# Seven half-size block products in the place of eight in the down projections of two MLPs

## The chip, the cores and the metric

One Trainium2 chip, one core of it. The metric is device time in microseconds (us), the median of the runs. The engines are named as the profile names them: PE is TensorE (PEld its weight loads), DVE is VectorE, ACT is ScalarE, POOL is GpSimd, SP is the engine that issues the DMAs.

## What is computed

Two decoder layers over 512 tokens of width 1024, all in float32. Each layer ends with an MLP of hidden width 4096, and a layer norm behind it:

```python
def sqrelu_mlp(x, w_up, w_down):
    return jnp.square(jax.nn.relu(x @ w_up)) @ w_down
...
        x = layer_norm(ALPHA * x + mix, ln_gain[layer, 0], ln_bias[layer, 0])
        x = layer_norm(ALPHA * x + sqrelu_mlp(x, mlp_w_up[layer], mlp_w_down[layer]), ln_gain[layer, 1], ln_bias[layer, 1])
```

Attention and its projections stand before the MLP; the change does not touch their arithmetic.

## The kernel before, in words

A matrix product of two float32 matrices is made of three: each operand is split as `hi + lo` (`hi` is the value rounded to float32r by ScalarE, `lo = value - hi` by VectorE or GpSimd), and PE adds `hi*hi`, `hi*lo` and `lo*hi` up in one bank of PSUM. A bank holds 128 partitions x 512 float32; there are four tags of two banks each (`g`, `o`, `s`, `t`).

Weights come from DRAM in units of 128 x 1024 numbers (512 KB): `unit` (L131) loads one into `wraw` (two buffers), ScalarE writes `whi` (L145), VectorE writes `wlo` (L146; in the attention parts GpSimd does it, by `lo_engine`). `whi` and `wlo` have four buffers each.

The MLP (`mlp`, L363) works in two halves of the hidden width. In a half, eight chunks of 256 hidden columns are computed by `tr_block` (L183): the weights are loaded into PE and the 512 tokens are the moving side, so a matmul is 512 wide (L191 to L193), and its output has the hidden columns on partitions. ScalarE applies relu (L377), VectorE squares (L378), ScalarE and VectorE split the result into `hh` and `hl` (L114, L116). Then the down projection goes over four chunks of 256 output columns: `hh` or `hl` of 128 tokens is loaded into PE and the weights are the moving side, 256 wide (L396 to L398). VectorE adds each finished bank to the residual `y` (L403, L405). The last chunk of the second half is computed token block by token block, each followed by its layer norm (`layer_norm`, L205), so that norm and output of one block run beside the matmuls of the next.

The order of the work on each engine is set by a scheduler of the framework from the program; every engine works its own queue in that order. A tile that takes the buffer of an older one waits until the older one's readers are done.

Of the kernel before, what the change touches and what calls it, by code (L numbers as in the profile page):

```python
# [8 lines left out]
F32 = mybir.dt.float32  # L9
F32R = mybir.dt.float32r  # L10
AF = mybir.ActivationFunctionType
ALU = mybir.AluOpType
# [40 lines left out]
# offsets in the tile of constants  # L53
# [7 lines left out]
def tile_trunk(ctx: ExitStack, tc: tile.TileContext, x, xt_in, ln_gain, ln_bias, w_up, w_down, w_ie, w_oe, lam_p, subln,  # L61
# [50 lines left out]
    def split(src, hi, lo, scale=1.0):  # L112
        """hi + lo = scale * src, exactly; hi and lo are float32r"""
# [15 lines left out]
    lo_engine, rope_engine = [V], [V]  # L129

    def unit(flat, off, nk, w, pl=None, parts=1):  # L131
        """one [128 nk x w] block of a weight matrix as hi and lo [128, nk, w]"""
# [5 lines left out]
        if pl is None:  # L138
            hi = new(wp, "whi", [P, UW], F32R, bufs=4)
            lo = new(wp, "wlo", [P, UW], F32R, bufs=4)  # L140
        else:
            hi, lo = pl[:, :UW], pl[:, UW:]
        for a in range(0, n, n // parts):
            c = slice(a, a + n // parts)
            A.activation(hi[:, c], raw[:, c], AF.Copy)  # L145
            lo_engine[0].tensor_tensor(lo[:, c], raw[:, c], hi[:, c].bitcast(F32), op=ALU.subtract)  # L146
        return (hi[:, :n].rearrange("p (k c) -> p k c", k=nk), lo[:, :n].rearrange("p (k c) -> p k c", k=nk))

    class Weights:
# [3 lines left out]
        def take(self, w, pl=None, nk=4, parts=1):  # L153
            u = unit(self.flat, self.off, nk, w, pl, parts)
# [3 lines left out]
        def chunk(self, w, *pls, parts=1):  # L158
            """all 8 row blocks of w columns: list of (hi, lo) [128, w]"""
            r = []  # L160
            for i, nk in enumerate((4, 4) if w <= 256 else (3, 3, 2)):
                h, l = self.take(w, pls[i].rearrange("p a c -> p (a c)") if pls else None, nk=nk, parts=parts)
# [3 lines left out]
    def nat_chunk(us, w, evac):  # L166
        """[512 x w] = x @ W chunk, tokens on partitions; evac(bank view [128, n, w], first token block, n)"""
# [15 lines left out]
    def tr_block(us, nb, cuts=(0, SEQ)):  # L183
        """[128 x 512] = (x @ W)^T for the nb-th 128 columns of a chunk"""
# [45 lines left out]
    def stacks_q(ap, b, scale):  # L230
        """from [128 = two heads x 64, 512]: per head the stack of hi and lo parts"""
# [766 lines left out]
```

## Time and profile before

| what | us |
|---|---|
| median of 3 runs | 1328.76 |
| the runs | 1325.63, 1328.76, 1329.45 |
| span of the profiled execution | 1325.2 |
| PE busy in it | 1288.5 |
| DVE busy | 735.7 |
| ACT busy | 557.1 |
| POOL busy | 302.1 |
| four down stretches, 92 each | 368 |

The profiled execution has no time of its own beside its span; the runs, which include what lies around the span, are 0.4 to 4.2 us longer than it. Busy time of PE is from its matmuls' modelled ends, which overlap: the pace of PE is read from the starts of successive matmuls, not from the mean duration of one. For DVE likewise: where two instructions stand without a wait between them, the second starts some 0.08 us before the first one's end.

### The profile page before, as it was taken

The page shows a single profiled execution, that of the slowest core. Times are in us where ns is not written, and L with a number is a line of the kernel's source. Part 1 is how long each engine was busy: PE and PEld are TensorE (multiplying, and loading weights), DVE is VectorE, ACT ScalarE, POOL GpSimd, SP SyncE. Part 2 cuts the span into 40 slices and gives each one's busy share as a digit, 9 for nine tenths or more (in the row PEclk, how much of TensorE's full clock was granted, in tenths as well). Part 3 has the DMA queues.
Part 4 walks back from the last instruction along what each step waited for, and adds up shares of the span by engine and source line. Part 5 has one row for each costly group of instructions (what it writes and reads, how often), then busy time and mean ns, then how long its engine had stood idle before and what let it go on. Part 6 is the DMA issues. An engine that isn't in the chain of part 4 may idle for free.

```text
span 1325.2 us, 21558 instructions
## 1 busy us (share of the span) xinstructions
PE 1288.5 (97%) x8726; PEld 1188.8 (90%) x8726; DVE 735.7 (56%) x1466; ACT 557.1 (42%) x1049; POOL 302.1 (23%) x321
## 2 busy tenths in 40 slices
PE   8999998999999999999999999999999999999997
PEld 7999896988888999889997888989988899888997
DVE  4467778787544233443347788877944422344334
ACT  5257767753344112332213566765334311233220
POOL 1135554454000000000034445555500000000003
PEclk9999998999999999999999999999999999999999
DMA  7321011212322222222323323242323232223321
GB/s 273 121 80 49 33 48 33 95 61 84 111 97 96 93 84 95 96 96 96 123 78 128 97 82 94 89 151 65 130 87 102 96 96 90 85 95 96 101 92 64
DMA packets 38578, 125.35 MB, mean 95 GB/s; under 512 B 4672, under 2 KB 5184, under 8 KB 38480
## 3 DMA queue, kind: packets, MB, share of 16 engines
q1 hardware_dynamic: 38480, 123.99, 28.2%
q8 instruction: 68, 1.11, 0.4%
q14 instruction: 30, 0.25, 0.1%
HBM read 119.75 MB, written 4.23 MB: 94 GB/s over the span
## 4 chain that ended last, share of the span: by engine, by line
PE 88%; DVE 7%; ACT 2%; issue 1%; DMA 1%; POOL 1%; SPq 0%; DVEq 0%; ACTq 0%
PE g L193 11%; PE g L191 10%; PE g L192 10%; PE o L398 9%; PE o L397 9%; PE o L396 9%; PE g L178 4%; PE g L179 4%; PE g L180 4%; PE t L285 3%; PE s L267 2%; PE s L268 2%; PE o L301 1%; PE o L300 1%; PE g L353 1%; PE t L550 1%
## 5 line engine op out<-in xcount | busy, mean ns | idle before, releaser
L145 ACT ACTIVATE whi<-wraw 128x1024 fp32r<-128x1024 f32 (+2 forms) x180 | 188.5, 1049 | 288.4 <-PE o L398 223.4
L146 DVE TENSOR_TENSOR wlo<-wraw,whi 128x1024 fp32r<-128x1024 f32 (+1 forms) x129 | 158.7, 1231 | 213.7 <-ACT whi L145 213.7
L398 PE MATMUL o<-whi,hl 128*128 128x256 f32 x928 | 262.3, 283 | 0.0
L397 PE MATMUL o<-wlo,hh 128*128 128x256 f32 x928 | 262.2, 283 | 0.0
L396 PE MATMUL o<-whi,hh 128*128 128x256 f32 x928 | 261.0, 283 | 0.0
L192 PE MATMUL g<-big,wlo 128*128 128x512 f32 x608 | 237.5, 391 | 0.0
L191 PE MATMUL g<-big,whi 128*128 128x512 f32 x608 | 237.3, 390 | 0.0
L193 PE MATMUL g<-big,whi 128*128 128x512 f32 x608 | 237.2, 390 | 0.0
L146 POOL TENSOR_TENSOR wlo<-wraw,whi 128x1024 fp32r<-128x1024 f32 (+2 forms) x51 | 123.7, 2430 | 429.3 <-ACT whi L145 417.0
L397 PEld LDWEIGHTS o<-wlo,hh 128*128 128x128 f32 x928 | 178.2, 192 | 0.2
L398 PEld LDWEIGHTS o<-whi,hl 128*128 128x128 f32 x928 | 178.2, 192 | 0.0
L396 PEld LDWEIGHTS o<-whi,hh 128*128 128x128 f32 x928 | 177.4, 192 | 0.2
L193 PEld LDWEIGHTS g<-big,whi 128*128 128x128 f32 x608 | 114.2, 188 | 23.6
L191 PEld LDWEIGHTS g<-big,whi 128*128 128x128 f32 x608 | 114.2, 188 | 23.1 <-issue 0.2
L192 PEld LDWEIGHTS g<-big,wlo 128*128 128x128 f32 x608 | 114.1, 188 | 23.0
L178 PE MATMUL g<-whi,big 128*128 128x256 f32 (+2 forms) x416 | 120.4, 289 | 0.8 <-DVE fz L809 0.4
L180 PE MATMUL g<-whi,big 128*128 128x256 f32 (+2 forms) x416 | 119.5, 287 | 0.0
L179 PE MATMUL g<-wlo,big 128*128 128x256 f32 (+2 forms) x416 | 119.1, 286 | 0.0
L378 DVE TENSOR_TENSOR h<-h 128x512 f32<-128x512 f32 x64 | 44.3, 692 | 125.5 <-ACT h L377 125.5
L272 ACT ACTIVATE p<-p,sm 128x128 f32<-128x128 f32 (+3 forms) x160 | 89.2, 558 | 46.8 <-DVE sm L271 45.6
L377 ACT ACTIVATE h<-g 128x512 f32<-128x512 f32 x64 | 38.2, 597 | 164.8 <-PE g L193 164.8
L210 POOL TENSOR_TENSOR ve<-ve,nhalf 128x1 f32<-128x1 f32 x16 | 15.9, 992 | 361.2 <-DVE ve L209 361.2
(249 smaller groups left out, 2530.3 us busy)
## 6 DMA issues: line engine op xcount, KB each, us to landing
wraw<-w_up SPq DMA_DIRECT2D x64, 512.0 KB, 3.3
wraw<-w_down SPq DMA_DIRECT2D x64, 512.0 KB, 3.3
wraw<-w_io SPq DMA_DIRECT2D x22, 512.0 KB, 3.5
wraw<-w_ie SPq DMA_DIRECT2D x18, 512.0 KB, 3.7
v<-w SPq DMA_DIRECT2D x8, 512.0 KB, 5.2
wraw<-w_oe SPq DMA_DIRECT2D x8, 512.0 KB, 3.5
cb<-c_dram SPq DMA_DIRECT2D x16, 256.0 KB, 3.3
wraw<-w_oo SPq DMA_DIRECT2D x8, 512.0 KB, 3.6
```

The source lines that it names most:

```text
L145: A.activation(hi[:, c], raw[:, c], AF.Copy)
L146: lo_engine[0].tensor_tensor(lo[:, c], raw[:, c], hi[:, c].bitcast(F32), op=ALU.subtract)
L178: T.matmul(bv[:, tt], xh, h, start=first, stop=False)
L179: T.matmul(bv[:, tt], xh, l, start=False, stop=False)
L180: T.matmul(bv[:, tt], xl, h, start=False, stop=last)
L191: T.matmul(b[:, a:e], h[:, cs], xh, start=k == 0, stop=False)
L192: T.matmul(b[:, a:e], l[:, cs], xh, start=False, stop=False)
L193: T.matmul(b[:, a:e], h[:, cs], xl, start=False, stop=k == 7)
L272: A.activation(pv, pv, AF.Exp, bias=sm[:, i:i + 1], scale=-1.0, accum_out=sm[:, 4 + i:5 + i])
L396: T.matmul(bvs[t], hh[:, ts_], us[0][:, f], start=first, stop=False)
L397: T.matmul(bvs[t], hh[:, ts_], us[1][:, f], start=False, stop=False)
L398: T.matmul(bvs[t], hl[:, ts_], us[0][:, f], start=False, stop=lst)
```

## The change

The hidden width is now worked in four groups of 1024 columns (two blocks `m` of 512) in the place of two halves. In a group, the product `hidden (512 tokens x 1024) @ W (1024 x 1024)` is cut in 2 x 2: tokens 0-255 and 256-511, the first and second 256 hidden columns of each block `m`, output columns 0-511 and 512-1023. The eight half-size block products that this takes become seven, each of a sum or difference of blocks of the hidden values (`left`) and a sum of blocks of the weights (`right`), and the seven results are added to and subtracted from the four quarters of `y` (`evac`). A half-size product is 24 matmuls, each 512 wide on the weights' side. Products are named by their number in the code, in the order 3, 5, 7, 6, 1, 2, 4.

The hidden values stay unsplit in a tile of the tag `big`; every product has its left side split anew (`hsplit`), and its right side (`wsplit`). Raw weights are kept in a new tag `wdr` (eight buffers, the whole of a group), loaded in pieces of 512. GpSimd forms the sums of weights, some of the updates of `y`, and the `lo` of every second unit of the up weights; nothing else of the up projection is changed but the buffers of its first chunk. The last group leaves products 2 and 4 to the end, norms tokens 0-255 ahead of them and 256-511 behind them.

```diff
     def mlp(mp, wu, wd, us0, ln, last):
...
+                us = us0 if m == 0 and j == 0 else wu.chunk(256, engs=(V, G))
...
-                    split(h, hh, hl)
-                    hT.append((hh, hl))
...
+        def wsplit(r):
+            hi = new(wp, "whi", [P, UW], F32R, bufs=4)
+            lo = new(wp, "wlo", [P, UW], F32R, bufs=4)
+            A.activation(hi, r, AF.Copy)
+            V.tensor_tensor(lo, r, hi.bitcast(F32), op=ALU.subtract)
...
+            def left(r):
+                hi = new(mp, "sh", [P, 2, 2, 256], F32R, bufs=3)
+                lo = new(mp, "sl", [P, 2, 2, 256], F32R, bufs=3)
+                for m in range(2):
+                    (h11, h12), (h21, h22) = H[m]
+                    if r == 5:
+                        src = new(mp, "t1", [P, 2, 256], bufs=1)
+                        V.tensor_tensor(src, h12, h11, op=ALU.subtract)
+                    elif r == 7:
+                        src = t3[m] = new(mp, "t3", [P, 2, 256], bufs=2)
+                        V.tensor_tensor(src, h22, h12, op=ALU.subtract)
...
+                    hsplit(hi[:, m], lo[:, m], src)
...
+            def right(r):
...
+                    if r == 5:
+                        src = new(mp, "wds", [P, UW], bufs=2)
+                        G.tensor_tensor(src, w["21", m], w["22", m], op=ALU.add)
+                    elif r == 7:
+                        src = w["22", m]
+                        G.tensor_tensor(src, src, w["12", m], op=ALU.add)
+                    elif r == 6:
+                        src = w["21", m]
+                        G.tensor_tensor(src, src, w["22", m], op=ALU.add)
+                    elif r == 1:
+                        src = w["21", m]
+                        G.tensor_tensor(src, src, w["11", m], op=ALU.add)
...
+            def product(r, lf, us, tt):
...
+                        T.matmul(bv, hh, us[m][0][:, k], start=first, stop=False)
+                        T.matmul(bv, hh, us[m][1][:, k], start=False, stop=False)
+                        T.matmul(bv, hl, us[m][0][:, k], start=False, stop=lst)
...
+                elif r == 6:
+                    e, f = ef[tt]
+                    V.tensor_tensor(f, f, b, op=ALU.add)
+                    V.tensor_tensor(e, e, b, op=ALU.subtract)
+                    G.tensor_tensor(y12, y12, f, op=ALU.add)
+                    add(y22, f, eng=G)
+                    add(y11, e, eng=G)
...
+            for r in (3, 5, 7, 6, 1) if end else (3, 5, 7, 6, 1, 2, 4):
+                lf, us = left(r), right(r)
+                for tt in range(2):
+                    evac(r, product(r, lf, us, tt), tt)
...
+        for g in range(4):
+            hs = [up(2 * g + m) for m in range(2)]
+            down(g, hs, g == 3)
```

In the first group of a layer `add` gives the updates of `y22` and `y11` to VectorE in the place of GpSimd, since they carry the factor ALPHA.

What this makes of the queues is shown at three places. First VectorE's queue in a down projection. Before, in layer 0 (`wlo` is the low part of a weight unit, `big` the residual, `o` a bank):

```order
L146 TENSOR_TENSOR wlo_5200<-wraw_5197,whi_5199 128x1024
L146 TENSOR_TENSOR wlo_5254<-wraw_5251,whi_5253 128x1024
L403 SCALAR_TENSOR_TENSOR big_3658<-big_3658,o_4919 128x256 x2
L403 SCALAR_TENSOR_TENSOR big_3661<-big_3661,o_4920 128x256 x2
L146 TENSOR_TENSOR wlo_5308<-wraw_5305,whi_5307 128x1024
L146 TENSOR_TENSOR wlo_5368<-wraw_5365,whi_5367 128x1024
L146 TENSOR_TENSOR wlo_5422<-wraw_5419,whi_5421 128x1024
L146 TENSOR_TENSOR wlo_5476<-wraw_5473,whi_5475 128x1024
L403 SCALAR_TENSOR_TENSOR big_3658<-big_3658,o_5141 128x256 x2
```

Now, in layer 1, group 1, from the second half of product 6's update to the last weight split of the down projection (`f`, `e` are sums of products, `sl` the low part of a left side, `wdr` raw weights or their sum, `t` a bank):

```order
L501 TENSOR_TENSOR f_10899<-f_10899,o_10987 128x512
L502 TENSOR_TENSOR e_10846<-e_10846,o_10987 128x512
L411 TENSOR_TENSOR sl_11092<-t_1938_10903,sh_11091 128x512
L411 TENSOR_TENSOR sl_11092<-t_1939_10907,sh_11091 128x512
L406 TENSOR_TENSOR wlo_11018<-wdr_10789,whi_11017 128x1024
L406 TENSOR_TENSOR wlo_11056<-wdr_10799,whi_11055 128x1024
L406 TENSOR_TENSOR wlo_11060<-wdr_10801,whi_11059 128x1024
L406 TENSOR_TENSOR wlo_11100<-wdr_10795,whi_11099 128x1024
L508 TENSOR_TENSOR big_9252<-big_9252,t_11021 128x512
L508 TENSOR_TENSOR big_9252<-big_9252,t_11035 128x512
L406 TENSOR_TENSOR wlo_11104<-wdr_10797,whi_11103 128x1024
```

Before, four units of weights and two pairs of updates took turns; now there are sums, splits of left sides, splits of weights and updates in one row, and the last weight split (row 11) stands behind two updates that wait for PE and for GpSimd.

Second GpSimd's queue, in the same group and up to the next up projection (L455 forms the right side of product 1, L503 and L481 update `y`, L446 and L449 form right sides of the next group, L146 is the low part of an up unit). Before, GpSimd had nothing to do in an MLP until its final layer norm:

```order
L455 TENSOR_TENSOR wdr_10789<-wdr_10789,wdr_10801 128x1024
L503 TENSOR_TENSOR big_9252<-big_9252,f_10884 128x512
L481 TENSOR_TENSOR big_9255<-big_9255,f_10884 128x512
L481 TENSOR_TENSOR big_9252<-big_9252,e_10830 128x512
L503 TENSOR_TENSOR big_9252<-big_9252,f_10899 128x512
L481 TENSOR_TENSOR big_9255<-big_9255,f_10899 128x512
L481 TENSOR_TENSOR big_9252<-big_9252,e_10846 128x512
L446 TENSOR_TENSOR wds_11473<-wdr_11401,wdr_11405 128x1024
L446 TENSOR_TENSOR wds_11479<-wdr_11403,wdr_11407 128x1024
L449 TENSOR_TENSOR wdr_11405<-wdr_11405,wdr_11409 128x1024
L449 TENSOR_TENSOR wdr_11407<-wdr_11407,wdr_11411 128x1024
L146 TENSOR_TENSOR wlo_11145<-wraw_11142,whi_11144 128x1024
```

The second half of the next group's first up unit is now split behind four sums for the next down projection.

Third PE's queue in the same group, from the second weight block of product 1 on (`t` is a bank of product 1, `s` of product 2, `o` of product 4; before, a down projection was 384 matmuls 256 wide, block by block, with no such heads drawn ahead):

```order
L469 MATMUL t_11021<-whi_11017,sh_11005 128x512
L469 MATMUL t_11035<-whi_11017,sh_11005 128x512
L469 MATMUL s_11063<-whi_11055,sh_11049 128x512
L469 MATMUL s_11077<-whi_11055,sh_11049 128x512
L469 MATMUL o_11107<-whi_11099,sh_11091 128x512
L469 MATMUL o_11121<-whi_11099,sh_11091 128x512
L470 MATMUL t_11021<-wlo_11018,sh_11005 128x512
L471 MATMUL t_11021<-whi_11017,sl_11006 128x512
L469 MATMUL t_11021<-whi_11017,sh_11005 128x512
```

First the heads of the second block of product 1 and of products 2 and 4 (six matmuls), then the rest of them: 54 matmuls from the first `wlo_11018` on. In the up projections PE's queue keeps its pattern of 24 matmuls per block.

## Rows read from the trace of the kernel before

**Rows 1.** page, busy us of each engine (share of the span) xinstructions

```profile
PE 1288.5 (97%) x8726; PEld 1188.8 (90%) x8726; DVE 735.7 (56%) x1466; ACT 557.1 (42%) x1049; POOL 302.1 (23%) x321
```

**Rows 2.** page, the chain that ended last, shares of the span by engine

```profile
PE 88%; DVE 7%; ACT 2%; issue 1%; DMA 1%; POOL 1%; SPq 0%; DVEq 0%; ACTq 0%
```

**Rows 3.** down, up: length, busy us PE PEld DVE ACT POOL, clock, DMA share

```profile
424.00:516.00 92.00, 92.00 (x768) 91.96 (x767) 26.18 (x32) 17.94 (x18) 0.00 (x0) 1.00 0.30 98
516.00:604.00 88.00, 88.00 (x394) 73.01 (x394) 40.50 (x48) 34.19 (x47) 0.00 (x0) 1.00 0.27 90
```

**Rows 4.** timeline of TensorE, an up projection: start us, us, line, op

```profile
399.68 0.39 PE L191 MATMUL g<-big,whi 128*128 128x512 f32 x1
...
401.04 0.39 PE L191 MATMUL g<-big,whi 128*128 128x512 f32 x1
```

**Rows 5.** timeline of TensorE, last up matmul, first matmuls of a down projection

```profile
423.94 0.39 PE L193 MATMUL g<-big,whi 128*128 128x512 f32 x1
424.16 0.28 PE L396 MATMUL o<-whi,hh 128*128 128x256 f32 x1
...
425.12 0.28 PE L398 MATMUL o<-whi,hl 128*128 128x256 f32 x1
```

**Rows 6.** groups by form, VectorE: xcount | busy us, mean ns | idle before

```profile
L146 DVE TENSOR_TENSOR wlo<-wraw,whi 128x1024 fp32r<-128x1024 f32 x126 | 155.6, 1236 | 211.1 <-ACT whi L145 211.1
L378 DVE TENSOR_TENSOR h<-h 128x512 f32<-128x512 f32 x64 | 44.3, 692 | 125.5 <-ACT h L377 125.5
```

**Rows 7.** groups by form, ScalarE

```profile
L145 ACT ACTIVATE whi<-wraw 128x1024 fp32r<-128x1024 f32 x174 | 183.6, 1057 | 271.7 <-PE o L398 214.1 <-PE g L193 25.3 <-PE g L180 7.0
L377 ACT ACTIVATE h<-g 128x512 f32<-128x512 f32 x64 | 38.2, 597 | 164.8 <-PE g L193 164.8
```

**Rows 8.** groups by form, GpSimd

```profile
L146 POOL TENSOR_TENSOR wlo<-wraw,whi 128x1024 fp32r<-128x1024 f32 x48 | 118.4, 2472 | 94.2 <-ACT whi L145 81.9 <-issue 12.4
L217 POOL TENSOR_TENSOR big<-big,lng 128x512 f32<-128x512 f32 x12 | 15.7, 1305 | 19.2 <-ACT big L216 19.2
```

**Rows 9.** timeline of VectorE beside and after two GpSimd instructions

```profile
328.54 0.69 DVE L358 BATCH_NORM_STATS2 st<-big 128x6 f32<-128x512 f32 x1
329.14 2.13 DVE L146 TENSOR_TENSOR wlo<-wraw,whi 128x1024 fp32r<-128x1024 f32 x1
331.19 0.68 DVE L116 TENSOR_TENSOR big<-t,big 128x512 fp32r<-128x512 f32 x1
331.79 0.67 DVE L357 TENSOR_TENSOR big<-big,g 128x512 f32<-128x512 f32 x1
...
333.59 1.20 DVE L146 TENSOR_TENSOR wlo<-wraw,whi 128x1024 fp32r<-128x1024 f32 x1
334.71 0.19 DVE L207 BATCH_NORM_AGGREGATE mv<-st 128x2 f32<-128x12 f32 x1
```

**Rows 10.** timeline of GpSimd in the same stretch

```profile
328.92 1.27 POOL L217 TENSOR_TENSOR big<-big,lng 128x512 f32<-128x512 f32 x1 [2.69 <-ACT big L216]
330.27 2.13 POOL L218 TENSOR_TENSOR big<-big,lnb 128x512 f32<-128x512 f32 x1
```

**Rows 11.** timeline of VectorE in layer 1, two SBUF inputs

```profile
738.98 2.67 DVE L829 SCALAR_TENSOR_TENSOR bias<-cb,cq,K 128x512 f32<-128x512 f32 x1
```

**Rows 12.** timeline of GpSimd in the same stretch

```profile
738.46 2.64 POOL L146 TENSOR_TENSOR wlo<-wraw,whi 128x1024 fp32r<-128x1024 f32 x1 [7.29 <-ACT whi L145]
```

**Rows 13.** two stretches in the attention of layer 0, columns as above

```profile
200.00:202.00 2.00, 0.06 (x1) 0.00 (x0) 2.00 (x1) 0.32 (x1) 2.00 (x2) 1.00 0.00 0
202.00:206.00 4.00, 3.65 (x15) 3.20 (x16) 3.31 (x11) 2.43 (x8) 2.52 (x1) 0.57 0.53 155
```

**Rows 14.** timeline of TensorE, last matmul

```profile
1317.61 0.28 PE L398 MATMUL s<-whi,hl 128*128 128x256 f32 x1
```

**Rows 15.** timeline of VectorE behind it

```profile
1317.92 0.42 DVE L405 TENSOR_TENSOR big<-big,s 128x256 f32<-128x256 f32 x1 [2.34 <-PE s L398]
...
1320.60 1.41 DVE L221 SCALAR_TENSOR_TENSOR big<-big,ve,lnb 128x512 f32<-128x512 f32 x2
```

More of the change, by code (lines that the diff above doesn't have):

```diff
@@ L129, in tile_trunk, with unit @@
     lo_engine, rope_engine = [V], [V]
-    def unit(flat, off, nk, w, pl=None, parts=1):
+    def unit(flat, off, nk, w, pl=None, parts=1, eng=None):
         n = nk * w
@@ L151, in __init__, with take, chunk @@
             self.flat, self.off = flat, 0
-        def take(self, w, pl=None, nk=4, parts=1):
-            u = unit(self.flat, self.off, nk, w, pl, parts)
+        def take(self, w, pl=None, nk=4, parts=1, eng=None):
+            u = unit(self.flat, self.off, nk, w, pl, parts, eng)
             self.off += P * nk * w
             return u
-        def chunk(self, w, *pls, parts=1):
+        def chunk(self, w, *pls, parts=1, engs=(None, None, None)):
             r = []
             for i, nk in enumerate((4, 4) if w <= 256 else (3, 3, 2)):
-                h, l = self.take(w, pls[i].rearrange("p a c -> p (a c)") if pls else None, nk=nk, parts=parts)
+                pl = pls[i] if pls else None
+                if pl is not None and not isinstance(pl, tuple):
+                    pl = pl.rearrange("p a c -> p (a c)")
+                h, l = self.take(w, pl, nk=nk, parts=parts, eng=engs[i])
                 r += [(h[:, k], l[:, k]) for k in range(nk)]
@@ L339, in out_proj @@
         us = [wo.take(256) for _ in range(4)]
-        us0 = wu.chunk(256, *[new(pl, "o", [P, 4, SEQ], F32R, bufs=2) for _ in range(2)])
+        us0 = wu.chunk(256, *[tuple(new(pl, tag, [P, 2, 2, 256], F32R, bufs=3).rearrange("p a b c -> p (a b c)")
+                                    for tag in ("sh", "sl")) for _ in range(2)])
         new_xT()
@@ L363, in mlp, with up @@
     def mlp(mp, wu, wd, us0, ln, last):
-        stats = [new(mp, f"mst{t}", [P, 24]) for t in range(NT)]
-        for hf in range(2):
-            hT = []
-            for c in range(8):
-                if hf == 0 and c == 1:
-                    lo_engine[0] = V
-                us = us0 if hf == 0 and c == 0 else wu.chunk(256)
+        stats = [new(mp, f"mst{t}", [P, 12]) for t in range(NT)]
+        wdv = wd.flat.rearrange("(h c f p j e) -> h f p c j e", h=2, c=4, f=4, p=P, j=2)
+        def up(m):
+            h = big()
+            for j in range(2):
+                us = us0 if m == 0 and j == 0 else wu.chunk(256, engs=(V, G))
@@ L371, in mlp @@
                 for nb in range(2):
[L372 removed]
+                    early = m == 0 and j == 0
                     b = tr_block(us, nb, (0, 384, 512) if early else (0, 512))
[L374 to L378 removed]
@@ new lines, in up, with raws @@
+                    hv = h[:, 2 * j + nb]
+                    A.activation(hv, b, AF.Relu)
+                    V.tensor_tensor(hv, hv, hv, op=ALU.mult)
+            return h
+        def raws(g):
+            w = {}
+            for q in ("21", "22", "12", "11"):
+                for m in range(2):
+                    r = new(mp, "wdr", [P, UW], bufs=8)
+                    f, j, jd = 2 * g + m, int(q[0]) - 1, int(q[1]) - 1
+                    nc.sync.dma_start(out=r.rearrange("p (c e) -> p c e", c=2),
+                                      in_=wdv[f // 4, f % 4, :, 2 * jd:2 * jd + 2, j])
+                    w[q, m] = r
+            return w
```

119 lines of the change are left out of this document (73 added, 46 removed).

## The prediction

> **What bounds the kernel now.** I read the page's first part, then its chain, then the stretches of the MLP, then single instructions. PE is busy for 1288.5 of 1325.2 us [rows 1], and the chain that ended last lies on PE for 88% [rows 2]. In a down stretch PE is busy for all of 92 us, with 768 matmuls at the full clock, and DVE for 26.2, ACT for 17.9, POOL for none [rows 3]; in an up stretch it is the same with DVE at 40.5 of 88. So in the MLPs nothing but PE counts today, and PE's pace is to be read from starts: a 512-wide matmul every 0.227 us (1.36 us for six) [rows 4], a 256-wide one every 0.120 us (0.96 for eight) [rows 5]. Between an up and a down projection PE loses nothing: the first down matmul starts 0.22 us after the last up one [rows 5].
>
> **PE's own work.** Removed: 4 x 768 = 3072 matmuls at 0.120 = 368.6 us. Added: 7 products x 24 x 4 groups x 2 layers = 1344 at 0.227 = 304.7 us. The gain is 63.9 us if PE never waits: a group's down projection takes 168 x 0.227 = 38.1 us in the place of 384 x 0.120 = 46.1. Both widths have a row, and these give a 512-wide matmul 13 ns, and a 256-wide one as many, above its columns at 2.4 GHz. The Trainium skill, TensorE: Matmul & The Clock Gate, section Back-to-back issue gap, puts that fixed part at 2.5 ns, which speaks against the wide form: by its 216 and 109 ns the gain would be an estimated 46 us. No row here has its 2.5 ns.
>
> **What DVE gets.** Per group's down projection 14 splits of left sides, 14 of weights (1024 wide), 8 differences and 18 updates. Back to back a 512-wide instruction starts 0.60 us after the one before, a 1024-wide one takes 1.13 (from 331.19 to 331.79, from 333.59 to 334.71) [rows 9]. That is 40 x 0.60 + 14 x 1.13 = 40 us against PE's 38.1, and a part can't be done ahead: the weights' buffers hold two products, and the left sides need the last square. So I followed one inner group's queues, with zero where its down projection starts:
> - DVE reaches the second weight split of product 7 at 10.9: its buffer is free when PE has issued all of product 3 (42 matmuls, 9.5 us), then ACT takes 1.06 [rows 7]. From there to the last split DVE has 9 splits of 1024 and 25 instructions of 512, and hardly a pause.
> - Eight of 512 and two of 1024 later (7.1) comes the first weight split of product 6: 18.0. PE has done 74 matmuls, 16.8, and waits.
> - The second one of product 6: 22.1. The first of product 1: 25.6. The second of product 1: six of 512 and one of 1024 later, 30.3.
> - Behind that PE has 54 matmuls, 12.2 us. The down projection ends at 42.6, not 38.1, for no other reason than DVE.
>
> **What POOL adds.** In the same stretch POOL now has two sums of 1024 (2.4 us each; the nearest row is L146's 2.47) and six updates of 512 (1.3 each) [rows 8]: 12.4 us. These are not beside DVE's work. At 329.14 a split that takes 1.23 alone took 2.13 while POOL ran L217, and POOL's L218, of the size of L217 (1.31), took 2.13 while the split ended [rows 6, 8 to 10]; in layer 1 a 512-wide DVE instruction took 2.67 us and ended 0.55 after POOL's L146 [rows 11, 12]. Both are DVE instructions with two SBUF inputs. With one input in PSUM DVE is not held: L116 and L357 took 0.68 and 0.67 under the same L218. Of DVE's instructions in a down projection, all splits and differences have two SBUF inputs, the updates from a bank have one. So a POOL instruction costs DVE its own length unless an update stands there:
> - sum 1 of product 1 falls between the two splits of product 6: +2.4; sum 2 behind them, where two updates cover half: +1.2;
> - of the six updates three fall ahead of product 1's second split: +3.8; the other three behind it, where PE still has its 54 matmuls to do: nothing on the path.
>
> That makes 30.3 + 7.4 = 37.7, and with 54 matmuls **50.0 us per inner down projection, 3.9 above the 46.1 of before**. The Trainium skill, SBUF — State Buffer, section Who interferes with whom, states it as an exclusive lock for the whole instruction, whoever comes first. By that alone all 12.4 us would be DVE's, 55.0 per down projection, and an estimated 1415 us in all; the rows with a PSUM input, which the same section exempts, are why I take 50.0.
>
> **The other terms.** The next up projection: behind its six updates POOL ends near 42.3 and has four sums and the split of the first chunk's second unit, 5 x 2.43 = 12.2, plus up to two DVE splits, so 56.8; PE wants that unit at 50.0 + 24 x 0.227 = 55.4. Lag 1.4 us, three times a layer. The first group has two updates on POOL and four on DVE: 49.4. Per layer: 3.3 + 3 x 3.9 + 3 x 1.4 = 19.2; both 38.4. The tail: after the last matmul [rows 14] DVE now has 7.7 us for the bank and two norms (about 12 instructions) where it had 4.1, from 1317.92 to 1322.0 [rows 15]; with their waits I take +4.4 at the end, and +2 between the layers, where the next projection begins with tokens that are ready. The first matmul of the MLP, the DMAs (before 0.30 of the engines' time [rows 3], the same bytes now, in pieces half as long) and ACT (38 of 95 us per group) I cost at nothing: their cover is PE's queue, and if the loads came late PE would wait at a chunk's start.
>
> Sum: 1325.2 + 38.4 + 6.4 = 1370.0 of span, 44.8 more; on the median of 1328.8, which is 3.6 over the span, **1374 us**. The bounds per down projection are 42.6 (POOL costs nothing) and 55.0 (all of it).
>
> **Rivals.**
> - *DVE and POOL run side by side* for this mix, or POOL's work falls where DVE waits anyway. Then 42.6 per down projection: 8 x -3.5 + 6.4 = -21.6, **1307**. It decides from 1.7 us of holds per group on: there 8 x (44.3 - 46.1) + 8.4 + 6.4 is zero. Against it speak rows 9 to 12; for it, that POOL's instants are inferred. 13%.
> - *All is hidden*: DVE gets ahead during the up projections. -63.9 + 6.4, **1271**. The buffers speak against it. 3%.
> - *The clock falls.* After PE had stood still from 200 to 202 its granted clock was 0.57 in the next 4 us, that is 1.2 GHz for most of it [rows 13]. Each group now has four waits of 1 to 7 us. One or two such stretches a group, each like that one (4 us x 0.43 / 0.5 = 3.4 us at half speed, 1.7 us of work lost), cost 1.7 to 3.4: 14 to 27 us, **1388 to 1401**. The Trainium skill, TensorE: Matmul & The Clock Gate, section A second HAM failure mode: psum-queue depth-cycling, tells of short idles between matmul groups that make the clock swing. PE stays over 75% busy here, and DVE sets the pace in these stretches. 25%.
>
> **How the numbers follow.** 54% for the forecast, from 1355 to 1387. What a measurement can tell from no change is 0.3%, 4 us. The first two rivals make faster 14% with a little of their spread within 0.3%; with cases between, 5% are within it, 81% slower. The range leaves out most of the faster cases and the end of the clock's: 1327 to 1408.
>
> **What would show it.** Right: PE's matmuls in the down stretches 1344, at 0.227 us; PE idle of 10 to 13 us per group, released by `wlo` (L406) of DVE; DVE nearly full in the down stretches; DVE splits of 2 to 3 us beside POOL's L455, L503, L481; POOL busy some 280 us more (64 sums, 30 splits, 40 updates). Wrong: L406 at 1.23 us throughout beside POOL, or PE waits below 6 us a group; and if PE's granted clock drops in every group, the third rival.

## The result, and the profile after

The changed kernel takes 1400.99 us (median of four runs, 1400.38 to 1401.88) where the kernel before takes 1329.11 beside it: the ratio is 1.055, 95% interval 1.053 to 1.057. It is **slower by 5.5%**, and 27 us slower than the 1374 forecast; the range held it. The profiled execution of 1401.88 us has a span of 1400.1.

The page of the changed kernel, busy time of the engines (before: [rows 1]) and the chain that ended last (before: [rows 2]):

```profile
PE 1273.6 (91%) x6998; PEld 1096.3 (78%) x6998; DVE 1033.4 (74%) x1668; ACT 638.5 (46%) x1161; POOL 623.3 (45%) x455
...
PE 63%; DVE 25%; issue 3%; DMA 3%; ACT 3%; POOL 2%; SPq 0%; DVEq 0%; ACTq 0%; POOLq 0%
```

PE has 1728 matmuls less, and its share of the chain falls from 88% to 63%; a quarter is DVE's now. POOL works twice as long. The next view gives the second down projection of layer 0 and the up projection behind it, the columns as in [rows 3]; then the three stretches around the MLPs (out projection to steady up projection, layer 0's last down matmul to steady attention, last matmul to the end), and in the last three rows the same stretches before:

```profile
484.95:532.76 47.81, 41.12 (x169) 32.39 (x168) 46.13 (x43) 20.98 (x27) 26.21 (x12) 0.96 0.28 88
532.76:578.61 45.85, 44.11 (x193) 35.90 (x192) 24.37 (x24) 14.98 (x19) 17.29 (x7) 1.00 0.29 93
...
328.70:352.40 23.70, 10.86 (x51) 9.71 (x50) 18.81 (x20) 6.24 (x9) 15.75 (x9) 0.64 0.38 133
720.90:751.40 30.50, 21.84 (x129) 20.42 (x129) 20.14 (x35) 10.40 (x17) 14.89 (x13) 0.72 0.35 122
1383.60:1400.10 16.50, 0.10 (x1) 0.00 (x0) 12.31 (x19) 2.44 (x3) 10.39 (x8) 0.61 0.33 128
...
329.00:342.20 13.20, 10.84 (x67) 10.03 (x65) 10.31 (x16) 3.96 (x6) 4.30 (x3) 1.00 0.66 212
694.30:712.00 17.70, 17.29 (x140) 16.90 (x139) 10.39 (x22) 7.30 (x13) 7.86 (x6) 1.00 0.41 135
1317.80:1325.20 7.40, 0.09 (x1) 0.00 (x0) 3.91 (x8) 0.00 (x0) 1.69 (x2) 0.77 0.28 106
```

A down projection takes 47.8 us, with PE idle for 6.7 and DVE busy for 46.1 of it. The three stretches took 13.2, 17.7 and 7.4 us before, and take 23.7, 30.5 and 16.5 now; in the first two PE is idle for 12.8 and 8.7 us, where it was for 2.4 and 0.4. The waits of PE in the whole span (line waited for, us in total, times, longest):

```profile
PE t L470 <- DVE wlo L406: 35.9, 16, 3.2
PE t L124 <- POOL big L221: 16.6, 3, 7.9
PE g L194 <- ACT big L387: 7.7, 4, 2.5
...
PE t L124 <- DVE big L116: 5.7, 2, 3.2
PE t L469 <- DVE e L498: 5.6, 8, 0.7
```

To see where the 74.9 us of span come from, both executions are cut at the same matmuls: the last one of an out projection, the first and last of each down projection (eight chunks of up projection before count as two times four, at 43.5 us for four):

| stage, us | before | forecast adds | after | added |
|---|---|---|---|---|
| to layer 0's out projection, end | 329.0 | 0 | 328.6 | -0.4 |
| out projection's end to the first down matmul, two layers | 103.0 | 0 | 129.5 | **26.5** |
| eight down projections | 370.8 | 30.0 | 382.2 | 11.4 |
| six up projections between them | 261.1 | 8.4 | 274.2 | 13.1 |
| layer 0's last down matmul to layer 1's out projection, end | 253.8 | 2.0 | 269.0 | **15.2** |
| last matmul to the end | 7.5 | 4.4 | 16.6 | 9.1 |
| span | 1325.2 | 44.8 | 1400.1 | 74.9 |

The down projections themselves lost less than forecast. What was not seen lies around them.

### The profile page after: what moved, and what is told of

Read it like the earlier page. It is cut to its first block, busy times and chain, and to the rows that moved or that the text cites. A ratio compares the mean times of both kernels' runs of the same rounds, so it can differ in the third digit from the quotient of the medians.

```text
span 1400.1 us, 18617 instructions
## 1 busy us (share of the span) xinstructions
PE 1273.6 (91%) x6998; PEld 1096.3 (78%) x6998; DVE 1033.4 (74%) x1668; ACT 638.5 (46%) x1161; POOL 623.3 (45%) x455
## 4 chain that ended last, share of the span: by engine, by line
PE 63%; DVE 25%; issue 3%; DMA 3%; ACT 3%; POOL 2%; SPq 0%; DVEq 0%; ACTq 0%; POOLq 0%
PE g L194 10%; PE g L195 10%; PE g L196 10%; DVE sl L411 6%; DVE wlo L406 5%; PE g L181 4%; PE g L183 4%; PE g L182 4%; PE t L288 2%; PE s L270 2%; DVE wlo L146 1%; PE s L271 1%; PE o L304 1%; PE o L470 1%; DMA wraw<-w_up 1%
## 5 line engine op out<-in xcount | busy, mean ns | idle before, releaser
L146 POOL TENSOR_TENSOR wlo<-wraw,whi 128x1024 fp32r<-128x1024 f32 (+1 forms) x81 | 197.9, 2446 | 261.6 <-ACT whi L145 249.2
L145 ACT ACTIVATE whi<-wraw 128x1024 fp32r<-128x1024 f32 (+3 forms) x120 | 125.3, 1046 | 186.8 <-DMA wraw<-w_up 110.3
L406 DVE TENSOR_TENSOR wlo<-wdr,whi 128x1024 fp32r<-128x1024 f32 x96 | 148.4, 1561 | 10.5 <-ACT whi L405 10.5
L405 ACT ACTIVATE whi<-wdr 128x1024 fp32r<-128x1024 f32 x96 | 99.7, 1054 | 100.4 <-PE t L471 70.4
L388 DVE TENSOR_TENSOR big<-big 128x512 f32<-128x512 f32 x64 | 64.4, 1011 | 97.9 <-ACT big L387 97.9
L455 POOL TENSOR_TENSOR wdr<-wdr,wdr 128x1024 f32<-128x1024 f32 x16 | 41.5, 2594 | 184.1 <-DVE wlo L406 184.1
L146 DVE TENSOR_TENSOR wlo<-wraw,whi 128x1024 fp32r<-128x1024 f32 (+2 forms) x39 | 66.9, 1717 | 63.0 <-ACT whi L145 63.0
L321 POOL TENSOR_TENSOR p<-p,rs 128x128 f32<-128x128 f32 (+2 forms) x108 | 71.3, 686 | 93.3 <-DVE rs L942 40.4
L470 PE MATMUL t<-wlo,sh 128*128 128x512 f32 x128 | 58.5, 457 | 35.9 <-DVE wlo L406 35.9
L387 ACT ACTIVATE big<-g 128x512 f32<-128x512 f32 x64 | 37.7, 596 | 101.5 <-PE g L196 101.5
L181 PEld LDWEIGHTS g<-whi,big 128*128 128x128 f32 x416 | 80.6, 194 | 3.8 <-ACT big L114 2.1
L183 PEld LDWEIGHTS g<-whi,big 128*128 128x128 f32 x416 | 80.6, 194 | 0.9 <-issue 0.4
```

Of the source, the lines that this page charges most:

```text
L146: (eng or lo_engine[0]).tensor_tensor(lo[:, c], raw[:, c], hi[:, c].bitcast(F32), op=ALU.subtract)
L181: T.matmul(bv[:, tt], xh, h, start=first, stop=False)
L183: T.matmul(bv[:, tt], xl, h, start=False, stop=last)
L405: A.activation(hi, r, AF.Copy)
L406: V.tensor_tensor(lo, r, hi.bitcast(F32), op=ALU.subtract)
```

## The experiments

Times are medians, ratios are to runs of the kernel before on the same chip (the changed kernel: 1.055). The stages of each profiled execution, cut as above (in e9 PE draws the first matmuls of a down projection into the up projection, so its two columns are one):

| kernel | us | ratio, 95% interval | starts | downs | ups | between | tail |
|---|---|---|---|---|---|---|---|
| changed | 1401.0 | 1.053 to 1.057 | 129.5 | 382.2 | 274.2 | 269.0 | 16.6 |
| e1_pin | 1365.9 | 1.028 to 1.031 | 101.6 | 386.3 | 260.2 | 272.4 | 16.8 |
| e2_vadd | 1390.2 | 1.046 to 1.049 | 131.1 | 383.0 | 258.7 | 270.1 | 20.2 |
| e4_fill | 1406.5 | 1.058 to 1.061 | 130.3 | 372.3 | 286.4 | 270.7 | 18.9 |
| e5_pin_vadd | 1352.7 | 1.015 to 1.019 | 101.9 | 370.1 | 258.4 | 272.6 | 19.8 |
| e6_pin_fill | 1341.1 | 1.008 to 1.011 | 101.7 | 359.3 | 260.2 | 269.7 | 18.8 |
| e7_no_pool | 1286.4 | 0.966 to 0.969 | 102.2 | 307.8 | 258.4 | 268.7 | 18.5 |
| e8_pin_plain | 1340.3 | 1.007 to 1.011 | 101.9 | 376.7 | 260.2 | 259.6 | 9.2 |
| e9_early | 1329.4 | 0.999 to 1.002 | 101.5 | 628.3 with the ups | | 259.3 | 9.3 |
| e12_idle_pool | 1385.2 | 1.042 to 1.045 | 138.0 | 347.1 | 272.8 | 273.5 | 20.4 |
| e3_wide | 1317.7 | 0.991 to 0.994 | 105.1 | 358.7 | 261.1 | 253.8 | 8.0 |
| e10_wide_runs | 1316.5 | 0.988 to 0.993 | 105.1 | 358.7 | 261.1 | 253.7 | 8.0 |
| e11_plain | 1315.5 | 0.989 to 0.992 | 102.4 | 349.1 | 261.1 | 262.3 | 8.8 |

### Four sums ahead of the norms

GpSimd's queue at the first start of the changed kernel (layer 0, out projection to up projection):

```profile
318.15 2.40 POOL L446 TENSOR_TENSOR wds<-wdr,wdr 128x1024 f32<-128x1024 f32 x1
320.50 1.76 POOL L221 TENSOR_TENSOR big<-big,lnb 128x512 f32<-128x512 f32 x1
322.23 2.39 POOL L446 TENSOR_TENSOR wds<-wdr,wdr 128x1024 f32<-128x1024 f32 x1
324.58 0.55 POOL L213 TENSOR_TENSOR ve<-ve,nhalf 128x1 f32<-128x1 f32 x1
325.10 5.38 POOL L449 TENSOR_TENSOR wdr<-wdr,wdr 128x1024 f32<-128x1024 f32 x2
330.44 1.53 POOL L213 TENSOR_TENSOR ve<-ve,nhalf 128x1 f32<-128x1 f32 x1
331.94 1.26 POOL L220 TENSOR_TENSOR big<-big,lng 128x512 f32<-128x512 f32 x1
333.17 2.34 POOL L146 TENSOR_TENSOR wlo<-wraw,whi 128x1024 fp32r<-128x1024 f32 x1
335.47 1.70 POOL L221 TENSOR_TENSOR big<-big,lnb 128x512 f32<-128x512 f32 x1
```

The raw weights of group 0 have landed, so the four sums for products 5 and 7 stand among the steps of the out projection's norms (L213, L220, L221), though their products start only at 394.6 and later. The norm's L221 that ends at 337.2 is the one that PE's transposes wait for (L124, 7.9 us, in the waits above). e1 puts the four sums behind what stands before them in the program, in every group:

```diff
-                        G.tensor_tensor(src, w["21", m], w["22", m], op=ALU.add)
+                        tc.keep_in_program_order(G.tensor_tensor(src, w["21", m], w["22", m], op=ALU.add))
...
-                        G.tensor_tensor(src, src, w["12", m], op=ALU.add)
+                        tc.keep_in_program_order(G.tensor_tensor(src, src, w["12", m], op=ALU.add))
```

> Only POOL's place of the sums for products 5 and 7 changes: they stand behind the norms' steps and behind all splits of the up projections' units, in every group. Theory (these sums in POOL's queue hold the norms before each MLP, +14 and +12 us there, and the unit splits of the next up projections, +14 us in all): the time from the out projection's end to the steady up projection falls back to that of before within 5 us per layer, the ups lose their waits of 1.6 to 2.5 us, the downs stay at 47 to 49 us, the boundary and the end stay: 1361 to 1376 us. Rival (the late start comes from the fallen clock or from the unit splits that POOL took over): 1393 to 1401.

1365.9 us. The starts fell from 129.5 to 101.6, where before has 103.0, the ups from 274.2 to 260.2. The same first stretch of e1, columns as above:

```profile
328.70:352.40 23.70, 21.58 (x142) 19.95 (x141) 12.18 (x18) 6.38 (x9) 8.52 (x5) 1.00 0.42 134
```

PE does 142 matmuls there in the place of 51, at a clock of 1.00 in the place of 0.64: the fall of the clock came with the waits and went with them. So 42 of the 75 us were a matter of where four instructions per group stand in POOL's queue; some 8 of them came back in the downs, half a microsecond each, and between the layers.

### POOL's updates

e2 gives the updates of `y` that POOL makes to DVE; e5 does it on top of e1.

```diff
-                    eng.tensor_tensor(y, y, p, op=op)
+                    V.tensor_tensor(y, y, p, op=op)
...
-                    G.tensor_tensor(y12, y12, f, op=ALU.add)
+                    V.tensor_tensor(y12, y12, f, op=ALU.add)
```

> The six updates of the output that POOL does per group (groups 1 to 3; two in group 0) go to DVE: POOL has 7.8 us less per group, DVE 3.6 us more. Theory (a POOL instruction holds DVE's instructions with two SBUF inputs, and the updates stand ahead of the sums and of the next unit splits): the last two weight splits of product 1 take 1.2 to 1.3 us in the place of 2.3, the downs fall by 1 to 3 us each, the waits in the ups get shorter: 1375 to 1391 us. Rival (DVE and POOL run side by side, and DVE's queue alone sets the pace): DVE's queue is 1.8 to 3.6 us longer per group, 1405 to 1425.

1390.2 us is in the theory's range, but mostly not for its reason: the first three downs of a layer rose to between 48.5 and 49.6 us, and what fell were the ups, by 15.5, nearly as in e1. Only the last down of a layer, which no next group's sums follow, did as the theory said: 44.5 us where it had 48.6 and 47.8. In the others POOL, free earlier, began the next group's sums inside the down projection, and held DVE with these: one DVE update took 2.9 us beside the first.

> The places of the sums as in e1_pin and the updates on DVE as in e2_vadd. In e2_vadd POOL, freed of the updates, started the next group's sums inside the down projections, so that they still held DVE; here they can't. Theory (a POOL instruction beside DVE's splits costs DVE more than the work that it takes off DVE): the downs fall from 48.7 us in e1_pin to 46 to 48, 1344 to 1362 us in all. Rival (DVE's queue alone counts, six instructions of 0.6 us more): 49.5 to 52 us each, 1372 to 1390.

1352.7 us: without sums to put there, downs of 45.5 to 47.6 where e1 had 46.1 to 48.8, 16 us less in all. Six instructions taken from POOL gain more than the same six cost on DVE. Two of its downs, the second group of either layer, also give the price of the clock, for they do the same work:

```profile
471.50:517.50 46.00, 40.05 (x172) 31.54 (x171) 44.22 (x55) 20.99 (x27) 11.86 (x4) 1.00 0.32 102
1107.40:1155.00 47.60, 41.67 (x171) 32.65 (x170) 44.24 (x55) 21.16 (x28) 11.50 (x4) 0.96 0.33 103
```

With a granted clock of 1.00 it takes 46.0 us, with 0.96 it takes 47.6: 1.6 us more PE time, 1.6 us longer.

### All of POOL's part, and its part without the results

e7 leaves out the sums (for each of products 5, 7, 6 and 1) and POOL's updates:

```diff
-                        src = new(mp, "wds", [P, UW], bufs=2)
-                        G.tensor_tensor(src, w["21", m], w["22", m], op=ALU.add)
+                        src = w["21", m]
...
-                        G.tensor_tensor(src, src, w["11", m], op=ALU.add)
...
-                    G.tensor_tensor(y12, y12, f, op=ALU.add)
-                    add(y22, f, eng=G)
-                    add(y11, e, eng=G)
+                    if g == 0:
+                        add(y22, f, eng=G)
+                        add(y11, e, eng=G)
```

> The changed kernel without POOL's part in the down projections: the eight sums of weights per group are left out (raw weights go to the splits in their place) and so are the updates that POOL makes; PE's, DVE's and ACT's instructions stay as they are. Theory (DVE's queue alone gives 42.6 us per down projection, as the prediction worked it out, and POOL the rest): downs of 42.6 to 44.5 us, no lag in the ups, starts as in e1_pin, 1318 to 1337 us. Rival (DVE's queue alone already takes 47 to 48, holds don't count): 1355 to 1366.

1286.4 us, below both: the downs take 38.5 us, PE's own 38.1, without a wait. VectorE in the second one of layer 0 (at 461.6):

```profile
479.50 2.35 DVE L406 TENSOR_TENSOR wlo<-wdr,whi 128x1024 fp32r<-128x1024 f32 x2
481.77 0.68 DVE L477 TENSOR_TENSOR big<-big,t 128x512 f32<-128x512 f32 x1
482.36 0.68 DVE L494 TENSOR_TENSOR e<-e,t 128x512 f32<-128x512 f32 x1
482.96 1.28 DVE L411 TENSOR_TENSOR sl<-big,sh 128x512 fp32r<-128x512 f32 x2
484.17 2.35 DVE L406 TENSOR_TENSOR wlo<-wdr,whi 128x1024 fp32r<-128x1024 f32 x2
486.44 0.68 DVE L497 TENSOR_TENSOR f<-f,o 128x512 f32<-128x512 f32 x1
```

and in the changed kernel's, which starts at 485.0:

```profile
500.46 3.50 DVE L411 TENSOR_TENSOR sl<-big,sh 128x512 fp32r<-128x512 f32 x2
...
505.08 1.21 DVE L406 TENSOR_TENSOR wlo<-wdr,whi 128x1024 fp32r<-128x1024 f32 x1
...
507.41 2.51 DVE L411 TENSOR_TENSOR sl<-big,sh 128x512 fp32r<-128x512 f32 x2
509.84 1.21 DVE L406 TENSOR_TENSOR wlo<-wdr,whi 128x1024 fp32r<-128x1024 f32 x1
510.98 0.68 DVE L501 TENSOR_TENSOR f<-f,o 128x512 f32<-128x512 f32 x1
...
513.37 3.15 DVE L411 TENSOR_TENSOR sl<-t,sh 128x512 fp32r<-128x512 f32 x2
516.44 6.73 DVE L406 TENSOR_TENSOR wlo<-wdr,whi 128x1024 fp32r<-128x1024 f32 x3
```

with POOL beside it:

```profile
500.02 2.78 POOL L455 TENSOR_TENSOR wdr<-wdr,wdr 128x1024 f32<-128x1024 f32 x1 [19.44 <-DVE wlo L406]
506.37 2.40 POOL L455 TENSOR_TENSOR wdr<-wdr,wdr 128x1024 f32<-128x1024 f32 x1 [3.57 <-DVE wlo L406]
511.73 1.30 POOL L503 TENSOR_TENSOR big<-big,f 128x512 f32<-128x512 f32 x1 [2.96 <-DVE f L501]
```

Two things differ. Beside POOL the pairs of left splits (L411) take 3.5, 2.5 and 3.2 us in the place of 1.3, and a weight split of the last group 2.2 on average in the place of 1.2. And product 1's sums (L455) wait for product 6's splits, since they are made in place of its blocks (their release is DVE's L406); the second split of product 1, the first instruction of the last group above, stands behind four updates and two more left splits and starts 31.5 us into the down projection. In e7, where nothing is to be summed, it is the first of the pair at 484.17, 22.6 us in, and the updates come after it. Of the 8.9 us between the two starts, 5.3 are the longer pairs of left splits, and 3.6 the four updates and the pair that now stand ahead (six times 0.60). To tell the two causes apart, e12 gives e7 POOL's work back, with results that nobody reads (its two sums of product 1 read a left side of product 6, `six`, so that they can't start earlier than that):

```diff
+                    if r in (5, 7, 6, 1):
+                        G.tensor_tensor(new(mp, "wds", [P, UW], bufs=2),
+                                        six[0] if r == 1 else w["21", m], w[{5: "22", 7: "12", 6: "22", 1: "11"}[r], m], op=ALU.add)
...
+                    for _ in range(1 if g == 0 else 3):
+                        G.tensor_tensor(new(mp, "wds", [P, UW], bufs=2)[:, :512], e, f, op=ALU.add)
```

> e7_no_pool with POOL's work put back as work that nobody waits for: per group eight sums of 1024 and six (two in group 0) of 512 columns into tiles that are never read; the raw weights go to the splits as in e7, and y12 in groups 1 to 3 gets no update. Theory (POOL's instructions cost by holding DVE and by standing in POOL's queue, whoever needs their results): the downs go from 38.5 us in e7 to 43 to 47, the starts are late by 8 to 14 us per layer again, 1345 to 1385 us. Rival (the cost lies in the sums' results coming late): downs of 38.5 to 40, 1286 to 1320 us.

1385.2 us, 0.2 above the theory's range, but the theory holds by halves. The starts came late again (138.0), though nobody waits for a sum: in the first of them PE waits 16.2 us for POOL's L221, with six sums ahead of it in the queue. The downs are not the theory's 43 to 47 us. The four inner groups have the rival's, the first group of a layer takes 54.5 and 53.2, the last one 42.2 and 40.9. The second and the first group of layer 0 (these windows end where the last matmul starts; by the table's cut they are 39.1 and 54.5):

```profile
494.90:533.70 38.80, 38.57 (x170) 31.63 (x169) 37.14 (x44) 21.11 (x27) 12.55 (x7) 1.00 0.23 76
397.30:451.60 54.30, 42.58 (x171) 33.81 (x170) 52.63 (x50) 21.10 (x27) 23.47 (x9) 0.84 0.26 79
```

The upper one, the second group, is half a microsecond longer than in e7 (38.5 by the table's cut), though POOL works for 12.6 us in it: POOL's instructions start 26 us in, when DVE has the splits of products 6 and 1 behind it and is ahead of PE. In the first group they start as late, but DVE still has four updates with two SBUF inputs (L481) and the left splits of product 4 ahead of the last weight split (VectorE of that group):

```profile
430.86 2.86 DVE L481 SCALAR_TENSOR_TENSOR big<-big,e 128x512 f32<-128x512 f32 x1
433.64 2.82 DVE L481 SCALAR_TENSOR_TENSOR big<-big,f 128x512 f32<-128x512 f32 x1
436.38 2.82 DVE L481 SCALAR_TENSOR_TENSOR big<-big,e 128x512 f32<-128x512 f32 x1
439.13 5.60 DVE L411 TENSOR_TENSOR sl<-t,sh 128x512 fp32r<-128x512 f32 x2
444.65 3.39 DVE L406 TENSOR_TENSOR wlo<-wdr,whi 128x1024 fp32r<-128x1024 f32 x1
```

POOL works on beside them without a pause, and PE waits 9.8 us for the left splits; its clock is at 0.84 in this stretch, which adds 4 us of PE time. So a hold by itself costs next to nothing; it costs where it stands ahead of a split that PE will wait for. In the changed kernel product 1's second split stands behind its late sums and behind such instructions.

### Filling the waits

e4 adds matmuls to the changed kernel where PE waits, e6 the same to e1:

```diff
+                    if r in (6, 1) and tt == 0 and m == 0:
+                        d = bank("g").rearrange("p (c e) -> p c e", c=2)
+                        for i in range(8):
+                            T.matmul(d, lf[0][:, 0, 0, ts_], us[0][0][:, 0], start=i == 0, stop=i == 7)
```

> The changed kernel with 16 matmuls more per group (8 behind the first half of product 6's first token block, 8 in product 1's) into a bank that nobody reads: 128 x 0.227 = 29 us of PE work, placed ahead of the waits. Theory (DVE's queue sets the end of product 1, PE's idle time and its slow stretches both lie in DVE's shadow): the downs stay within 1 us of 47 to 49 each, 1396 to 1408 us, with less PE idle and perhaps fewer slow stretches. Rival (the fallen clock in the downs costs its 1.7 to 3.4 us per group on the path): with the waits filled the slow stretches go and 10 to 20 us with them, 1380 to 1391. Rival (PE's work is what counts): 1425 to 1430.

> The places of the sums as in e1_pin and the 16 idle matmuls per group as in e4_fill. In e4_fill three of four downs fell from 47.8 to 45.3 us with no slow stretch in them, but the ups grew by as much, where POOL's queue was late; here POOL's queue is not late. Theory (a slow stretch behind DVE's last split of product 1 is on the path): the downs fall from 48.7 to 45.5 to 47 us, the ups stay at 43.5, 1340 to 1354 us. Rival (only the order of the matmuls mattered, or the fall comes back elsewhere): 1362 to 1372.

1406.5 and 1341.1 us: both totals are where the theory had them. But e4's came by another way, since its downs did not stay at 47 to 49 us: the first of a layer went to 51.7, the others to between 43.5 and 45.9. e6 is 25 us faster than e1 with 29 us of useless matmuls more. Neither measures the clock alone: with the longer PE work the scheduler also put DVE's instructions in another order. VectorE in the second down of e6 (it starts at 467.2):

```profile
493.15 3.48 DVE L406 TENSOR_TENSOR wlo<-wdr,whi 128x1024 fp32r<-128x1024 f32 x3
496.55 0.67 DVE L505 TENSOR_TENSOR f<-f,o 128x512 f32<-128x512 f32 x1
```

The second split of product 1 now follows the first, ahead of the four updates, 27.1 us into the down projection in the place of 32.5 in e1. That takes away most of the wait (PE is idle for 2.5 us of this down projection, in e1 for 7.7), and with it the fall of the clock; the two can't be parted here. In e4 the shorter downs (372.3) came back as longer ups (286.4), where PE waits 13.6 us in all for POOL's unit splits (L146): POOL's queue was as late as before.

### The last group

e8 undoes the last group of e1: eight plain products into eight banks, the last four weight units token block by token block.

```diff
+            for t in range(NT):
+                for u in todo[4:]:
+                    mmp(bs, t, *u)
+                for jd in range(2):
+                    y = Y_(t, jd)
+                    V.tensor_tensor(y, y, bs[t, jd], op=ALU.add)
+                    V.bn_stats(stats[t][:, jd * 6:(jd + 1) * 6], y)
+                layer_norm(mp, t, stats[t].rearrange("p (a b) -> p a b", b=6), *ln, last=last,
...
-            down(g, hs, g == 3)
+            if g == 3:
+                down_plain(g, hs)
+            else:
+                down(g, hs, False)
```

> The places of the sums as in e1_pin, and the last group of each layer undone: eight plain products 512 wide into eight banks, the last four weight units token block by token block, each with its norm behind it, as before. Theory (the longer way from the last matmul to the end, +9.5 us, and to layer 1's attention, about +17 in e1_pin, comes from the last group's form, where four norms stand together at the end of a full DVE queue): tail of 7 to 8 us, the last downs at 43.5 to 45, 1326 to 1340 us. Rival (norms, DVE's backlog of splits or the next projection's weights make it late whatever the form): 1350 to 1360.

1340.3 us, 0.3 above the theory's range: tail 16.8 to 9.2, between the layers 272.4 to 259.6, and the two last downs 44.5 and 43.5 in the place of 48.7. So seven products with two norms behind the last matmul cost 20 us at the two ends, and a plain group 512 wide is shorter than one of seven products with its waits.

e9 goes on from there: sums in the up projections, updates on DVE.

```diff
+            src = w[r, m] = w["22", m] if r == 7 else new(mp, "wds", [P, UW], bufs=5)
+            tc.keep_in_program_order(G.tensor_tensor(src, w[a, m], w[b, m], op=ALU.add))
...
+            w = sums(raws(g)) if g in (1, 2) else None
             hs.append(up(2 * g + 1))
```

> e8_pin_plain with POOL kept out of the down projections: all sums but one stand in the up projections (product 6's sum is product 5's plus one block, in buffers of their own, five in the place of two), and the updates are on DVE. e7_no_pool showed downs of 38.5 us with no POOL beside them. Theory (what the change lost in the downs is POOL's part, its holds and its late sums, and nothing else): the six downs by seven products fall from 48.7 us to 39 to 42, ups at 43.5 to 45, 1286 to 1306 us: faster than before and than the plain 512-wide products. Rival (the holds only move into the ups, where squares and splits then come late): ups of 46 to 50 or downs of 44 to 46, 1308 to 1335.

1329.4 us, ratio 0.999 to 1.002 to before: the rival. An up and a down projection together take 90 to 92 us, as in e8. A part of the wait has gone to the up projections, to POOL's own half of the unit splits behind the sums; the rest stays in the downs, behind DVE's splits:

```profile
PE g L195 <- POOL wlo L146: 12.1, 4, 3.4
PE o L462 <- DVE wlo L406: 10.1, 8, 2.9
```

### The width alone

e3 takes the kernel before and makes its plain products 512 wide; e10 has the weights' columns in two runs of 256, as the change has them; e11 uses e8's plain form in all groups.

```diff
-            for c in range(4):
-                end = hf == 1 and c == 3
...
+            for c in range(2):
+                end = hf == 1 and c == 1
+                bs = [bank(g) for g in ("ttgg", "ooss")[c]]
...
+                    us = wd.take(512, nk=2)
...
-                        us = wd.take(256)
```

> The kernel of before with one part of the change alone: down projections as plain products, no sums, with weights moving 512 wide (1536 matmuls in the place of 3072). Theory (the width by itself takes 13 ns off for each matmul that is saved; no DVE or POOL work is added): 1536 x 0.227 = 348.7 in the place of 368.6, 1309 us (1306 to 1312), ups and downs without waits. Rival (the first four banks of a down projection, or the weights' units, wait at a chunk's start): 1 us for each of 8 chunks or more, 1317 to 1325. By the Trainium skill, TensorE: Matmul & The Clock Gate, section Back-to-back issue gap, the fixed part is 2.5 ns and the estimate would be 1326.

> e3_wide with the moving weights laid out as the changed kernel has them: each matmul reads two runs of 256 columns in the place of one run of 512. In e3_wide a matmul took 0.233 us from start to start, in the changed kernel and in the up projections 0.227. Theory (the layout of the moving block makes the 6 ns): 0.227, 1536 x 0.006 = 9 us less, 1307 to 1310 us. Rival (it comes from the left sides or from the banks, which are as in e3_wide): 0.233 again, 1316 to 1319.

> All groups of both layers as the last group of e8_pin_plain: eight plain products 512 wide per 1024 hidden columns, four weight units for all tokens, then four token block by token block, into eight banks; no sum of weights, no difference, POOL with the splits of every second unit only. In e8's last group a matmul took 0.2266 us from start to start, in e3_wide and e10_wide_runs 0.233. Theory (what e3 lost lies in how its left sides or banks lie, not in the width): 1536 x 0.2266 = 348.1 in the place of 368.6, 1306 to 1311 us. Rival (a wait at each group's start for banks or left sides, as eight groups now each need all eight banks): 1 us or more a group, 1316 to 1325.

1317.7, 1316.5 and 1315.5 us: all three beat both kernels, before by 0.7 to 1.0%, little, but clear of noise by their intervals. e3's total is its rival's and e11's lies between its two ranges, but no waits at the starts of chunks or groups show in either. In e3 and e10 successive matmuls start 0.233 us apart on average (0.232 in the rows below), in e11 0.2266 (TensorE of e3, then of e11, six matmuls each from first to last row):

```profile
439.62 0.40 PE L393 MATMUL g<-whi,hl 128*128 128x512 f32 x1
...
441.01 0.40 PE L393 MATMUL t<-whi,hl 128*128 128x512 f32 x1
```

```profile
479.64 0.39 PE L460 MATMUL t<-whi,sl 128*128 128x512 f32 x1
...
481.00 0.39 PE L460 MATMUL g<-whi,sl 128*128 128x512 f32 x1
```

The moving side's layout is not the reason (e10); left sides, banks and the other engines' work beside them differ between e10 and e11, and which of them it is stays open. e11 has the downs that the width promised, 349.1 us for 1536 x 0.2266 = 348.1, but loses 8.5 us between the layers, where its waits were not followed up.

## Why the prediction was right in sign and 27 us short

- **PE's own work**: right. The seven products take 38.5 us when nothing holds them (e7). By the Trainium skill, TensorE: Matmul & The Clock Gate, section Back-to-back issue gap, whose formula for an isolated matmul has 2.5 ns beside the columns, the wide form would gain an estimated 4 us by itself (1536 matmuls fewer). By the Trainium skill's figures there the prediction's estimate of 46 us comes out at 45. e11's downs gained 21.7, and its 0.2266 us against before's 0.120 for half the width [rows 5] speaks against 2.5 ns for these matmuls.
- **DVE's queue**: the mechanism was right, its start was late. The second split of product 7 was put at 10.9 us, "when PE has issued all of product 3 (42 matmuls, 9.5 us)"; it started at 6.8. The count was right (in the second down projection, from 484.95 on, product 3's last matmul starts at 9.3), but the split took another buffer: ScalarE's half of it starts at 5.7, released by a matmul into bank `s`, which is product 5's:

```profile
490.65 1.06 ACT L405 ACTIVATE whi<-wdr 128x1024 fp32r<-128x1024 f32 x1 [1.14 <-PE s L471]
```

That is the 24th matmul, after 5.4 us, the last one that reads product 5's first weight block. All later instants come 3 to 4 us earlier than forecast: the second split of product 1 ends at 33.8 where the text had 37.7, and the 12.2 us of matmuls behind it then give 46.0. e7's 38.5 does not measure the text's 42.6 without POOL: with no sum to wait for, the scheduler orders DVE otherwise, and no run has the change's order without POOL.

- **POOL's holds**: right in kind, 7.4 us in the forecast. Up to that split the longer instructions in the changed kernel's second down add 6.4 us over the lengths that they have alone: 2.2, 1.2 and 1.9 in the three pairs of left splits, 1.1 in the weight split. POOL's instructions up to there take some 12 us. e12 adds the condition: only ahead of a split that PE waits for. The Trainium skill, SBUF — State Buffer, section Who interferes with whom, states the lock; the trace agrees with the lock (L406 takes 1.51 us on average in the changed kernel, 1.22 in e7) and not with charging DVE for all of it.
- **What would show it**: the 1344 matmuls at 0.227 us, the releases by `wlo` (L406), splits of 2 to 3 us beside POOL, and POOL's increase (321 us where some 280 stood) are there; PE's idle time per group is 5.1 to 6.7 us, where 10 to 13 stood and under 6 was to count against the forecast.
- **The clock**: the third rival happened in every down projection of the changed kernel, one or two falls each (0.96 above). Where PE has no wait left behind the fall, it costs the work lost, 1.6 us (e5's pair); with a wait behind it nothing shows: layer 0's third down projection, at 0.93 with two falls, takes 47.7 us, the second, at 0.96 with one, 47.8. The forecast of 50.0 per inner down thus came out at 47.8 by two errors: 4 too much from the queue, some 1.7 too little from the clock. That the total lies on this rival's 1401 is chance.
- **The first matmul of the MLP**: the step that failed. "I cost at nothing: their cover is PE's queue" looked at loads and ACT, and not at POOL's queue, where four sums could pass the norms. 26.5 us; e1 gives all of it back. POOL's order is fixed when the kernel is built; the prediction read it inside the MLP alone.
- **The lag of the ups**: 13.1 where 8.4 stood, from the four sums, as forecast (e1: ups back to 260.2), but not spread as forecast: nothing behind a layer's first group, then 2.8 us twice in layer 0 and 5 twice in layer 1. PE's wait there names ACT's relu (L387), not the unit's split; how the one leads to the other was not followed.
- **The tails**: mis-sized, 24.3 where 6.4 stood. At the end DVE works for 12.3 us behind the last matmul, where 7.7 were forecast. Counted were the bank and two norms; not counted was that the norms of the first two token blocks, no longer spread beside earlier matmuls, stand in the same full DVE queue, and that between the layers the next projection's transposes wait for them (e8, with the old form, gives 20 back).

## What to carry to other kernels

The sums, ready early, were put where POOL's queue had room, not where they harm least: when a change gives an engine new work, read that engine's whole order, also in stages that the change does not touch, and pin what nobody needs yet behind what somebody waits for. An algorithm that saves multiplications pays in additions, and here the additions' engines were two that hold each other up; the cheap half of the change, the wider moving side, is worth 12 us by itself, and the seven products in this form lost that and 72 us more.

## What the runs showed of the hardware that was not expected

- A plain matmul of the same size and width started every 0.2266 us in e11 and every 0.233 on average in e3 and e10, at the same granted clock of 1.00, with no wait shown.
- Sixteen useless matmuls per group made a kernel 25 us faster (e6 against e1), with another order on VectorE and a clock that no longer fell in the down projections.
- 12.6 us of GpSimd's work in a down projection cost half a microsecond (e12, second group: 39.1 against 38.5 in e7). In the first group 23.5 us of the same kind of work cost 16.0 (54.5), some 4 of them by TensorE's clock at 0.84, the rest by what stood in VectorE's queue beside it.
